# Attention logits and indexer scores computed for two heads per step, one head on each half of TensorE's rows

## The chip, the cores and the metric

One core of one Trainium2 chip runs the whole kernel. The metric is the device time of one launch in microseconds (us). TensorE (PE) multiplies, and its weight loads have a row of their own (PEld); VectorE (DVE), ScalarE (ACT) and GpSimd (POOL) do the rest, and SyncE (SP) issues the weight DMAs.

## The reference, cut to what matters

A trunk of two layers over 528 positions (16 meta tokens and 512 tokens) of width 1024, in float32. Layer 0 is RWKV-7 time mixing, layer 1 sparse attention; each is wrapped in two SwiGLU feed-forwards. The change is in layer 1 alone. There, `q` has 16 heads of 64, `k` and `v` 4 heads of 64, and a small indexer has 8 query heads `qi` of 64, one key `ki` and 8 weights `wi`:

```python
rel = relu(einsum("bqhd,bkd->bqhk", qi, ki))
score = einsum("bqh,bqhk->bqk", wi, rel)          # then causal mask
_, idx = top_k(score, 128)
logits = einsum("bqgrd,bqkgd->bqgrk", qg, kg) * 64 ** -0.5
p = softmax(logits over the 128 selected keys)
o = einsum("bqgrk,bqkgd->bqgrd", p, vg)
```

## The kernel before, in words

**The dense part.** Each weight block of 128 columns is split into a rounded part and a rest (`Weights.round` on ACT, `Weights.split` on DVE; tiles `whi` and `wlo`, 1024 columns at a time), each activation likewise, and a block product is three matmuls in a rounded format (`mm3`, line 496) into a bank of the tag `acc` (four buffers). The stages are generators that yield before each block; `ffn` (614), `kvq` (1545) and `ao` (1650) are such main streams.

**The side work.** Attention and the indexer run as side chains (`beside`, 711) that `run` (729) mixes into a main stream while the program is built. `Clock` (238) holds a time for every engine by a price list; a matmul of float32 operands is priced at four passes over its columns, one matmul after another. Before each main block `run` lets chains step whose inputs are due earlier, and after it chains that are ready, until TensorE's modelled time has grown by `share` = 400 ns, as long as the modelled DVE and ACT are no more than `FULL` ahead (1500 ns beside `kvqA` and `f10b`, 3000 ns beside `kvqB` and `f11a`, line 47 and 732). A chain that yields `("bg", a, b)` is ready when the next buffer of the tag `bg` and the tiles `a`, `b` are free in the model (`Clock.late`, 285): one buffer is looked at, the next. `drain` (750) steps chains that are left over when a main stream ends. The order so fixed is the order on the chip; each engine executes its own in order.

**Banks.** `bbank` (493) hands out PSUM banks for side work: tag `bg` in a ring of three, `ry` one.

**The indexer**, `select(i)` (1467), for the query block i = 0 to 3 of 128 tokens, with `Wd` = 144 + 128 i keys in two halves `s`: for each of 8 heads and each half, one yield, one float32 matmul of 64 rows (`qiT[i][half, c]` against `kiT[half, s]`; even heads lie on partitions 0 to 63, odd ones on 64 to 127, and `kiT` is on both) into one `bg` bank, a relu on ACT into `rel[:, s]`, and a multiply-add on DVE into `sc`. Then 16 rounds of max and replace on DVE make the selection, and `bias[i]`.

**Attention**, `attend(i)` (1570), i = 1 to 4, with `Wd` = 16 + 128 i keys: `logits(hh)` (1579) makes, for each segment of the keys (one, or two of 264 at i = 4), one float32 matmul of 64 rows into one `bg` bank, and a DVE operation that adds the bias out of the bank into `pr` and takes the minimum; then ACT takes the exponential. `divide(hh)` (1597) normalises on DVE. `turn(hh)` (1602) transposes the head's probabilities by TensorE into a `bg` bank (two of them at i = 4), and DVE and ACT copy them into `pt`. `values(g)` (1620) multiplies by V for four heads at once. The loop at line 1639 runs `logits(s)`, `divide(s - 1)`, `turn(s - 3)`, so a head is turned three heads after its logits.

**Where it runs.** `select(0)`, `select(1)` and `attend(1)`, `attend(2)` lie beside `kvqA` and the feed-forward `f10b`; `select(2)`, `select(3)`, `attend(3)`, `attend(4)` beside `kvqB` and `f11a` (lines 1695 to 1714). After each feed-forward comes `drain`, then `ao`, which needs attention's result.

Of the kernel before, what the change touches and what calls it, by code (L numbers as in the profile page):

```python
# [10 lines left out]
F32 = mybir.dt.float32  # L11
F32R = mybir.dt.float32r
I32 = mybir.dt.int32
AF = mybir.ActivationFunctionType
OP = mybir.AluOpType
# [4 lines left out]
T = 528  # L20
# [413 lines left out]
def trunk(ctx, tc, wall, units, h0, vec, cstd, gqk, out, stop=None, gap=0.0, share=400.0, slack=200.0, fulls={}):  # L434
    clock = Clock()
    nc = Core(tc.nc, clock)
    @contextmanager
    def tile_pool(name, bufs=1, **kw):
        with tc.tile_pool(name=name, bufs=bufs, **kw) as pool:
            yield Pool(pool, bufs, clock)  # L440
# [52 lines left out]
    def bbank(tag="bg"):  # L493
        return psum.tile([128, 512], F32, name=tag, bufs={"bg": 3, "ry": 1}[tag])
# [870 lines left out]
    at = ctx.enter_context(tile_pool("at"))  # L1365
# [24 lines left out]
    for q in ("cos", "sin"):  # L1390
        turns[2, q] = cst[q].rearrange("p (i e) -> p i e", e=16)
        for w in range(2):
            turns[w, q] = at.tile([128, 5, 16], F32, name=f"{q}{w}")
            nc.vector.tensor_tensor(turns[w, q], turns[2, q], gb[:, w:w + 1, 0:16].to_broadcast([128, 5, 16]),
                                    op=OP.mult)
    kT = at.tile([128, 4, T], F32, name="kT")
    V = at.tile([128, 5, 256], F32, name="V")
    kiT = at.tile([128, T], F32, name="kiT")
    qiT = {}
    wi = at.tile([128, 4, 8], F32, name="wi")  # L1400
    qT = {}
# [60 lines left out]
    def segments(Wd):  # L1462
        return [(0, Wd)] if Wd <= 512 else [(0, Wd // 2), (Wd // 2, Wd)]

    bias = {}

    def select(i):

        Wd = 144 + 128 * i
        sc = at.tile([128, T], F32, name="sc", bufs=1)  # L1470
        rel = at.tile([128, T], F32, name="rel", bufs=1)
        for hh in range(8):
            c, half = hh // 2, slice(64 * (hh % 2), 64 * (hh % 2) + 64)
            for s in (slice(0, Wd // 2), slice(Wd // 2, Wd)):
                yield "bg", qiT[i][half, c], kiT[half, s]
                p = bbank()[:, :Wd // 2]
                nc.tensor.matmul(p, qiT[i][half, c], kiT[half, s], start=True, stop=True)
                nc.scalar.activation(rel[:, s], p, AF.Relu)
                if hh == 0:
                    nc.vector.tensor_scalar(sc[:, s], rel[:, s], wi[:, i, 0:1], None, op0=OP.mult)  # L1480
                else:
                    nc.vector.scalar_tensor_tensor(sc[:, s], rel[:, s], wi[:, i, hh:hh + 1], sc[:, s],
                                                   op0=OP.mult, op1=OP.add)
        nc.vector.tensor_add(sc[:, Wd - 128:Wd], sc[:, Wd - 128:Wd], cst["causal"])
        wk = at.tile([128, T], F32, name="rel", bufs=1)
        m8 = at.tile([128, 8], F32, name="m8", bufs=1)
        for t in range(TOPK // 8):
            src = sc if t == 0 else wk
            nc.vector.max(m8, src[:, :Wd])
            nc.vector.match_replace(out=wk[:, :Wd], in_to_replace=m8, in_values=src[:, :Wd], imm_value=-2.0 * BIG)  # L1490
            yield -1500
        b = at.tile([128, T], F32, name=f"bias{i % 2}")
        nc.vector.tensor_scalar(b[:, :Wd], wk[:, :Wd], -1.5 * BIG, BIG, op0=OP.is_gt, op1=OP.mult)
        nc.vector.scalar_tensor_tensor(b[:, Wd - 128:Wd], cst["causal"], -1.0, b[:, Wd - 128:Wd],
                                       op0=OP.mult, op1=OP.max)
        bias[i] = b
# [73 lines left out]
    def attend(i, XO):  # L1570


        Wd = 16 + 128 * i
        nb = i + 1
        b = bias[i - 1]
        sm = at.tile([128, 16], F32, name="sm", bufs=1)
        pr, pt, po = {}, {}, {}

        def logits(hh):

            c, half, g = hh // 2, slice(64 * (hh % 2), 64 * (hh % 2) + 64), hh // 4
            lg = pr[hh] = at.tile([128, T], F32, name="pr", bufs=4)
            mn = at.tile([128, 2], F32, name="mn", bufs=4)
            sg = segments(Wd)
            for j, (s0, s1) in enumerate(sg):
                yield "bg", qT[i][half, c], kT[half, g, s0:s1]
                p = bbank()
                nc.tensor.matmul(p[:, :s1 - s0], qT[i][half, c], kT[half, g, s0:s1], start=True, stop=True)
                nc.vector.tensor_tensor_reduce(out=lg[:, s0:s1], in0=p[:, :s1 - s0], in1=b[:, s0:s1],
                                               scale=1.0, scalar=3e38, op0=OP.add, op1=OP.min,  # L1590
                                               accum_out=mn[:, j:j + 1])
            if len(sg) == 2:
                nc.vector.tensor_tensor(mn[:, 0:1], mn[:, 0:1], mn[:, 1:2], op=OP.min)
            nc.scalar.activation(lg[:, :Wd], lg[:, :Wd], AF.Exp, bias=mn[:, 0:1], scale=-1.0,
                                 accum_out=sm[:, hh:hh + 1])

        def divide(hh):
            r = sm[:, hh:hh + 1]
            nc.vector.reciprocal(r, r)
            nc.vector.tensor_scalar(pr[hh][:, :Wd], pr[hh][:, :Wd], r, None, op0=OP.mult)  # L1600

        def turn(hh):
            if hh % 4 == 0:
                pt[hh // 4] = at.tile([128, 5, 4, 128], F32, name="pt", bufs=1)
            to = pt[hh // 4][:, :, hh % 2 * 2 + hh % 4 // 2]
            for k0 in range(0, nb, 4):
                ks = range(k0, min(k0 + 4, nb))
                yield "bg", pr[hh][:, :Wd]
                p = bbank()
                pv = p.rearrange("p (m t) -> p m t", t=128)  # L1610
                for kb in ks:
                    t0, t1 = TOK[kb]
                    nc.tensor.transpose(pv[:t1 - t0, kb - k0], pr[hh][:, t0:t1], ident)
                if k0 == 0:
                    nc.vector.tensor_copy(to[:16, 0], pv[:16, 0])
                    nc.scalar.activation(to[:, 1:len(ks)], pv[:, 1:len(ks)], AF.Copy)
                else:
                    nc.scalar.activation(to[:, k0:k0 + len(ks)], pv[:, :len(ks)], AF.Copy)

        def values(g):  # L1620

            q, c0 = g // 2, 256 * (g % 2)
            yield "ry" if g % 2 == 0 else po[q][:, c0:c0 + 256], pt[g]
            if g % 2 == 0:
                po[q] = bbank("ry")
            for kb in range(nb):
                k = TOK[kb][1] - TOK[kb][0]
                for o in (0, 1):
                    nc.tensor.matmul(po[q][64 * o:64 * o + 64, c0:c0 + 256], V[:k, kb, 64 * g:64 * g + 64],
                                     pt[g][:k, kb, 2 * o:2 * o + 2].rearrange("p h t -> p (h t)"),  # L1630
                                     start=kb == 0, stop=kb == nb - 1)
            if g % 2:
                pv = po[q].rearrange("p (m t) -> p m t", t=128)
                s = slice(TOK[i][0] - XO.t0, TOK[i][1] - XO.t0)
                hi, lo = XO.hi[:, 4 * q:4 * q + 4, s], XO.lo[:, 4 * q:4 * q + 4, s]
                nc.scalar.activation(hi, pv, AF.Copy)
                nc.vector.tensor_sub(lo, pv, hi.bitcast(F32))

        for s in range(20):
            if s % 4 == 3 and s > 3:  # L1640
                yield from values(s // 4 - 1)
            if s < 16:
                yield from logits(s)
            if 0 <= s - 1 < 16:
                divide(s - 1)
            if 0 <= s - 3 < 16:
                yield from turn(s - 3)
        yield 0

    def ao(XO, r, nxt, X=None):  # L1650
# [21 lines left out]
    def attend_range(q, i, name):  # L1672
        while ("q", i + 1) not in have or i - 1 not in bias:
            yield None
        XO[q] = Split(xq, DT, q, name)
        yield from attend(i, XO[q])
        while i not in bias:
            yield None
        yield from attend(i + 1, XO[q])
# [15 lines left out]
    QI = tiles_of((1, 2, 0), "xb_hi")  # L1695
    run(early(idx(XS["xa"], QI, (0, 1, 2)), norms[3], B))
    beside(heads_chain(), chain(*(idx_heads(i, QI) for i in (0, 1, 2)), select(0), select(1)))
    beside(attend_range(QA, 1, "xa"))
    run(early(kvq(XS["xa"], (0, 1, 2)), norms[3], B, X=x_of(B, "xb"), start=40), "kvqA")
# [4 lines left out]
    QI = tiles_of((3, 4), "xa_hi")  # L1704
    run(early(idx(XS["xb"], QI, (3, 4)), norms[5], QA))
    beside(heads_chain(), chain(idx_heads(3, QI), idx_heads(4, QI), select(2), select(3)))
    beside(attend_range(QB, 3, "xb"))
    run(early(kvq(XS["xb"], (3, 4)), norms[5], QA, X=x_of(QA, "xa"), start=40), "kvqB")
# [63 lines left out]
```

## Time and profile before

| what | us |
|---|---|
| median of 3 runs | 2402.96 (2399.5 to 2404.71) |
| the profiled execution | 2405.28 |
| its span on the core | 2403.5 |
| TensorE matmul busy | 2335.7 |
| VectorE busy | 1706.2 |
| ScalarE busy | 1263.9 |

The profiled execution is one launch; its span runs from its first to its last instruction. A float32 matmul stands in the trace as two MATMUL records and two weight loads. Every operation is recorded under the line of one helper, L341, so tile names tell the groups apart: `bg<-kT,qT` is a logits matmul, `bg<-kiT,qiT` a score matmul, `bg<-ident,pr` a transpose of `turn`, `ry<-pt,V` one of `values`, and `acc<-...` the main stream. A MATMUL's duration reaches to its modelled end, so neighbours overlap; what a matmul costs TensorE is read from starts.

### The profile page before, as it was taken

How to read it: one execution, taken by the hardware profiler on the slowest of the kernel's cores; microseconds unless marked ns; L12 is line 12 of the kernel's file. 1: busy time of each engine (PE TensorE's matmuls, PEld its weight loads, DVE VectorE, ACT ScalarE, POOL GpSimd, SP SyncE). 2: the span in 40 equal slices, each digit the busy share in tenths (PEclk: the TensorE clock that was granted, in tenths of full speed). 3: DMA queues.
4: the chain of work that ended last, by engine and by line, in shares of the span. 5: the costliest groups of instructions: out<-in, count | busy, mean ns of one | idle time of the engine just before them, and what ended most of it. 6: DMA issues, size and time to landing. Idle time of an engine off the chain costs nothing.

```text
span 2403.5 us, 49406 instructions
## 1 busy us (share of the span) xinstructions
PE 2335.7 (97%) x20122; PEld 2189.8 (91%) x20122; DVE 1706.2 (71%) x3337; ACT 1263.9 (53%) x2125; POOL 169.5 (7%) x215
## 2 busy tenths in 40 slices
PE   8998999999889999999999999999999999999999
PEld 8997889998789899999999999799888888879999
DVE  7667888856787975576566566687767888666765
ACT  5443664456448535644444444456665546565543
POOL 0001521010043011000000000000000000000000
PEclk9999999999899999999999999999999999999999
DMA  6553335542334454244555555454434444425554
GB/s 228 174 177 114 125 125 172 172 133 72 106 115 159 153 164 133 81 132 153 176 176 167 186 190 177 140 168 142 150 122 138 141 144 133 139 78 168 177 185 141
DMA packets 101491, 356.13 MB, mean 148 GB/s; under 512 B 11520, under 2 KB 15632, under 8 KB 101264
## 3 DMA queue, kind: packets, MB, share of 16 engines
q1 hardware_dynamic: 99120, 347.91, 43.8%
q0 software_dynamic: 2144, 5.07, 0.8%
q8 instruction: 158, 2.59, 0.4%
q14 instruction: 69, 0.57, 0.1%
HBM read 348.60 MB, written 4.33 MB: 147 GB/s over the span
## 4 chain that ended last, share of the span: by engine, by line
PE 53%; DVE 2%; ACT 1%; issue 0%; DVEq 0%; ACTq 0%
PE acc L341 46%; PE bg L341 6%; PE ry L341 1%; DVE wlo L341 1%; DVE qst L341 0%; ACT whi L341 0%; DVE h L341 0%; DVE pr L341 0%; DVE tb L341 0%; DVE xa_lo L341 0%; DVE m L341 0%; DVE rel L341 0%; DVE nst L341 0%; DVE hid_lo L341 0%; ACT xa_hi L341 0%
## 5 line engine op out<-in xcount | busy, mean ns | idle before, releaser
L341 ACT ACTIVATE whi<-wraw 128x1024 fp32r<-128x1024 f32 (+1 forms) x658 | 688.5, 1051 | 465.2 <-PE acc L341 274.8
L341 DVE TENSOR_TENSOR wlo<-wraw,whi 128x1024 fp32r<-128x1024 f32 (+1 forms) x658 | 809.8, 1234 | 170.8 <-ACT whi L341 170.1
L341 PE MATMUL acc<-hid_hi,whi 128*128 128x256 f32 (+1 forms) x1408 | 412.1, 293 | 6.0 <-DVE h L341 5.9
L341 PE MATMUL acc<-hid_lo,whi 128*128 128x256 f32 (+1 forms) x1408 | 399.5, 284 | 0.0
L341 PE MATMUL acc<-hid_hi,wlo 128*128 128x256 f32 (+1 forms) x1408 | 399.4, 284 | 0.0
L341 PE MATMUL acc<-xa_hi,whi 128*128 128x256 f32 (+1 forms) x1088 | 316.4, 291 | 1.8 <-ACT xa_hi L341 1.4
L341 PE MATMUL acc<-x_hi,whi 128*128 128x272 f32 (+1 forms) x1024 | 303.1, 296 | 8.7 <-ACT whi L341 6.2
L341 PE MATMUL acc<-xa_hi,wlo 128*128 128x256 f32 (+1 forms) x1088 | 309.0, 284 | 0.1
L341 PE MATMUL acc<-xa_lo,whi 128*128 128x256 f32 (+1 forms) x1088 | 308.9, 284 | 0.1
L341 PE MATMUL acc<-x_hi,wlo 128*128 128x272 f32 (+1 forms) x1024 | 294.9, 288 | 0.5 <-DVE wlo L341 0.5
L341 PE MATMUL acc<-x_lo,whi 128*128 128x272 f32 (+1 forms) x1024 | 294.5, 288 | 0.1
L341 PEld LDWEIGHTS acc<-hid_hi,whi 128*128 128x128 f32 x1408 | 265.5, 189 | 23.0 <-issue 12.2
L341 PEld LDWEIGHTS acc<-hid_lo,whi 128*128 128x128 f32 x1408 | 266.9, 190 | 0.2 <-DVE hid_lo L341 0.2
L341 PEld LDWEIGHTS acc<-hid_hi,wlo 128*128 128x128 f32 x1408 | 265.8, 189 | 0.0
L341 PEld LDWEIGHTS acc<-xa_hi,whi 128*128 128x128 f32 x1088 | 206.2, 190 | 19.7 <-issue 17.1
L341 PE MATMUL acc<-xb_hi,whi 128*128 128x256 f32 x752 | 215.4, 286 | 0.0
L341 PE MATMUL acc<-xb_lo,whi 128*128 128x256 f32 x752 | 210.7, 280 | 0.0
L341 PE MATMUL acc<-xb_hi,wlo 128*128 128x256 f32 x752 | 210.6, 280 | 0.0
L341 PEld LDWEIGHTS acc<-x_hi,whi 128*128 128x128 f32 x1024 | 194.9, 190 | 15.2 <-ACT whi L341 6.2
L341 PEld LDWEIGHTS acc<-xa_lo,whi 128*128 128x128 f32 x1088 | 206.6, 190 | 0.6 <-DVE xa_lo L341 0.5
L341 PEld LDWEIGHTS acc<-xa_hi,wlo 128*128 128x128 f32 x1088 | 206.2, 190 | 0.4 <-DVE wlo L341 0.4
L341 PEld LDWEIGHTS acc<-x_hi,wlo 128*128 128x128 f32 x1024 | 194.7, 190 | 1.0 <-DVE wlo L341 1.0
(295 smaller groups left out, 4440.4 us busy)
## 6 DMA issues: line engine op xcount, KB each, us to landing
wraw<-wall SPq DMA_DIRECT2D x644, 512.0 KB, 3.3
wraw<-wall SPq DMA_DIRECT2D x10, 438.0 KB, 3.3
out<-h SPq DMA_DIRECT2D x8, 256.0 KB, 2.3
h<-h SPq DMA_DIRECT2D x2, 512.0 KB, 8.7
ynat<-L POOLq DMA_DIRECT2D x2, 512.0 KB, 4.4
T<-ynat POOLq DMA_DIRECT2D x2, 512.0 KB, 4.2
L<-gm POOLq DMA_DIRECT2D x14, 64.0 KB, 2.8
gm<-T POOLq DMA_DIRECT2D x4, 224.0 KB, 6.8
```

Of the source, the lines that this page charges most:

```text
L341: r = f(*args, **kw)
```

## The change

`select` handles two heads `2c`, `2c + 1` per step and half of the keys: one yield (on both heads' rows), two banks, the two matmuls one right behind the other, then two relus and two multiply-adds. The relus write two slots of `rel` by head, no longer by half of the keys. `logits(c)` does the same for two heads and each segment: one yield, two banks, two matmuls, two DVE operations; then minima and exponentials of both. The loop of `attend` runs over 8 pairs: `logits(c)`, `divide` of both heads of c - 1, `turn` of both heads of c - 1, and `values` after every second pair. The rings (three `bg` banks, four `pr` and `mn` buffers), the price list and the yields' check of one next buffer stay.

```diff
+        w = Wd // 2
+        for c in range(4):
+            for s in (slice(0, w), slice(w, Wd)):
+                yield "bg", qiT[i][:, c], kiT[:, s]
+                ps = [bbank()[:, :w] for _ in range(2)]
+                for o in (0, 1):
+                    half = slice(64 * o, 64 * o + 64)
+                    nc.tensor.matmul(ps[o], qiT[i][half, c], kiT[half, s], start=True, stop=True)
+                for o in (0, 1):
+                    hh, r = 2 * c + o, rel[:, o * w:(o + 1) * w]
+                    nc.scalar.activation(r, ps[o], AF.Relu)
...
-        def logits(hh):
+        def logits(c):
...
+            for o in (0, 1):
+                pr[2 * c + o] = at.tile([128, T], F32, name="pr", bufs=4)
+                mn[o] = at.tile([128, 2], F32, name="mn", bufs=4)
             for j, (s0, s1) in enumerate(sg):
-                yield "bg", qT[i][half, c], kT[half, g, s0:s1]
-                p = bbank()
-                nc.tensor.matmul(p[:, :s1 - s0], qT[i][half, c], kT[half, g, s0:s1], start=True, stop=True)
-                nc.vector.tensor_tensor_reduce(out=lg[:, s0:s1], in0=p[:, :s1 - s0], in1=b[:, s0:s1],
-                                               scale=1.0, scalar=3e38, op0=OP.add, op1=OP.min,
-                                               accum_out=mn[:, j:j + 1])
+                yield "bg", qT[i][:, c], kT[:, g, s0:s1]
+                ps = [bbank()[:, :s1 - s0] for _ in range(2)]
+                for o in (0, 1):
+                    half = slice(64 * o, 64 * o + 64)
+                    nc.tensor.matmul(ps[o], qT[i][half, c], kT[half, g, s0:s1], start=True, stop=True)
+                for o in (0, 1):
+                    nc.vector.tensor_tensor_reduce(out=pr[2 * c + o][:, s0:s1], in0=ps[o], in1=b[:, s0:s1],
+                                                   scale=1.0, scalar=3e38, op0=OP.add, op1=OP.min,
+                                                   accum_out=mn[o][:, j:j + 1])
...
-        for s in range(20):
-            if s % 4 == 3 and s > 3:
-                yield from values(s // 4 - 1)
-            if s < 16:
-                yield from logits(s)
-            if 0 <= s - 1 < 16:
-                divide(s - 1)
-            if 0 <= s - 3 < 16:
-                yield from turn(s - 3)
+        for c in range(9):
+            if c % 2 and c > 1:
+                yield from values(c // 2 - 1)
+            if c < 8:
+                yield from logits(c)
+            if c:
+                for hh in (2 * c - 2, 2 * c - 1):
+                    divide(hh)
+                for hh in (2 * c - 2, 2 * c - 1):
+                    yield from turn(hh)
+        yield from values(3)
```

## Rows read from the trace of the kernel before

**Rows 1.** The page: the span, and busy time, share and count of each engine.

```profile
span 2403.5 us, 49406 instructions
...
PE 2335.7 (97%) x20122; PEld 2189.8 (91%) x20122; DVE 1706.2 (71%) x3337; ACT 1263.9 (53%) x2125; POOL 169.5 (7%) x215
```

**Rows 2.** Busy time by stretch: start:end, length, then PE, PEld, DVE, ACT, POOL.

```profile
1962.00:1982.00 20.00, 20.00 (x91) 12.39 (x90) 12.43 (x23) 8.59 (x21) 0.00 (x0) 1.00 0.29 97
...
1520.00:1811.00 291.00, 288.50 (x2071) 252.31 (x2070) 213.18 (x560) 177.05 (x320) 0.10 (x1) 0.99 0.42 141
1860.00:2187.00 327.00, 323.40 (x2200) 266.75 (x2199) 245.71 (x594) 188.59 (x324) 0.00 (x0) 1.00 0.39 127
```

**Rows 3.** Tile views of qT, then qiT: count, ns min/median/max, starts, forms.

```profile
L341 PE MATMUL bg<-kT,qT x160: 282/438/601, 1642.8 to 2169.2; 64*128 64x264 f32 x64, 64*128 64x144 f32 x32, 64*128 64x272 f32 x32, 64*128 64x400 f32 x32
...
L341 PE MATMUL bg<-kiT,qiT x128: 272/329/487, 1526.8 to 1981.4; 64*128 64x72 f32 x32, 64*128 64x136 f32 x32, 64*128 64x200 f32 x32, 64*128 64x264 f32 x32
```

**Rows 4.** Timeline of PE, one logits matmul of 144 columns: start, us, instruction.

```profile
1642.23 0.28 PE L341 MATMUL acc<-xb_hi,wlo 128*128 128x256 f32 x1
...
1642.58 0.28 PE L341 MATMUL acc<-xb_hi,wlo 128*128 128x256 f32 x1
1642.79 0.51 PE L341 MATMUL bg<-kT,qT 64*128 64x144 f32 x2
...
1643.45 0.28 PE L341 MATMUL acc<-xb_lo,whi 128*128 128x256 f32 x1
```

**Rows 5.** Timeline of PE, one logits matmul of 400 columns.

```profile
1990.84 0.28 PE L341 MATMUL acc<-xa_hi,wlo 128*128 128x256 f32 x1
1991.04 0.94 PE L341 MATMUL bg<-kT,qT 64*128 64x400 f32 x2
...
1992.13 0.28 PE L341 MATMUL acc<-xa_lo,whi 128*128 128x256 f32 x1
```

**Rows 6.** Timeline of PE, two logits matmuls of 400 columns in a row.

```profile
2000.35 0.28 PE L341 MATMUL acc<-xa_hi,wlo 128*128 128x256 f32 x1
2000.55 0.94 PE L341 MATMUL bg<-kT,qT 64*128 64x400 f32 x4
...
2001.65 0.28 PE L341 MATMUL acc<-xa_lo,whi 128*128 128x256 f32 x1
```

**Rows 7.** Timeline of PE, two score matmuls of one head, 136 columns each.

```profile
1624.06 0.28 PE L341 MATMUL acc<-xb_hi,wlo 128*128 128x256 f32 x1
1624.27 0.73 PE L341 MATMUL bg<-kiT,qiT 64*128 64x136 f32 x4
...
1625.15 0.28 PE L341 MATMUL acc<-xb_lo,whi 128*128 128x256 f32 x1
```

**Rows 8.** Groups of ACT and DVE, 1520 to 2190: busy us, mean ns, idle before.

```profile
L341 ACT ACTIVATE whi<-wraw 128x1024 fp32r<-128x1024 f32 (+1 forms) x171 | 177.9, 1047 | 49.3 <-PE acc L341 32.9 <-DVE q L341 5.5 <-issue 4.5
...
L341 ACT ACTIVATE pt<-bg 128x384 f32<-128x384 f32 (+2 forms) x80 | 28.8, 382 | 35.2 <-DVE pt L341 32.5 <-DVE sm L341 2.0
L341 ACT ACTIVATE rel<-bg 128x72 f32<-128x72 f32 (+3 forms) x64 | 19.3, 311 | 30.5 <-PE bg L341 27.5 <-DVE bias L341 2.4
...
L341 DVE TENSOR_TENSOR wlo<-wraw,whi 128x1024 fp32r<-128x1024 f32 (+1 forms) x170 | 205.6, 1213 | 24.4 <-ACT whi L341 24.3
L341 DVE CUSTOM_DVE_ANT_0 pr<-bg,bias 128x264 f32<-128x264 f32 (+3 forms) x80 | 34.7, 434 | 41.0 <-PE bg L341 40.9
```

**Rows 9.** Waits of PEld, 1520 to 2190: total us, times, longest.

```profile
PEld bg L341 <- DVE mn L341: 1.8, 6, 0.6
PEld bg L341 <- ACT pt L341: 1.1, 3, 0.5
```

**Rows 10.** Timeline of PE: the last `values` before `ao`, and the first block of `ao`.

```profile
1807.10 1.66 PE L341 MATMUL ry<-pt,V 16*64 16x256 f32 x12
...
1811.27 0.28 PE L341 MATMUL acc<-xa_hi,whi 128*128 128x256 f32 x1
```

More of the change, by code (lines that the diff above doesn't have):

```diff
@@ L1471, in select @@
         rel = at.tile([128, T], F32, name="rel", bufs=1)
[L1472 to L1483, printed above, removed]
+        w = Wd // 2
[9 more added lines that the diff above has]
+                    nc.scalar.activation(r, ps[o], AF.Relu)
+                    if hh == 0:
+                        nc.vector.tensor_scalar(sc[:, s], r, wi[:, i, 0:1], None, op0=OP.mult)
+                    else:
+                        nc.vector.scalar_tensor_tensor(sc[:, s], r, wi[:, i, hh:hh + 1], sc[:, s],
+                                                       op0=OP.mult, op1=OP.add)
         nc.vector.tensor_add(sc[:, Wd - 128:Wd], sc[:, Wd - 128:Wd], cst["causal"])
@@ L1577, in attend @@
         pr, pt, po = {}, {}, {}
-        def logits(hh):
-            c, half, g = hh // 2, slice(64 * (hh % 2), 64 * (hh % 2) + 64), hh // 4
-            lg = pr[hh] = at.tile([128, T], F32, name="pr", bufs=4)
-            mn = at.tile([128, 2], F32, name="mn", bufs=4)
+        def logits(c):
+            g = c // 2
+            mn = {}
+            for o in (0, 1):
+                pr[2 * c + o] = at.tile([128, T], F32, name="pr", bufs=4)
+                mn[o] = at.tile([128, 2], F32, name="mn", bufs=4)
             sg = segments(Wd)
             for j, (s0, s1) in enumerate(sg):
-                yield "bg", qT[i][half, c], kT[half, g, s0:s1]
-                p = bbank()
-                nc.tensor.matmul(p[:, :s1 - s0], qT[i][half, c], kT[half, g, s0:s1], start=True, stop=True)
-                nc.vector.tensor_tensor_reduce(out=lg[:, s0:s1], in0=p[:, :s1 - s0], in1=b[:, s0:s1],
-                                               scale=1.0, scalar=3e38, op0=OP.add, op1=OP.min,
-                                               accum_out=mn[:, j:j + 1])
[L1592 to L1595, printed above, removed]
+                yield "bg", qT[i][:, c], kT[:, g, s0:s1]
[7 more added lines that the diff above has]
+                                                   accum_out=mn[o][:, j:j + 1])
+            for o in (0, 1):
+                lg = pr[2 * c + o]
+                if len(sg) == 2:
+                    nc.vector.tensor_tensor(mn[o][:, 0:1], mn[o][:, 0:1], mn[o][:, 1:2], op=OP.min)
+                nc.scalar.activation(lg[:, :Wd], lg[:, :Wd], AF.Exp, bias=mn[o][:, 0:1], scale=-1.0,
+                                     accum_out=sm[:, 2 * c + o:2 * c + o + 1])
         def divide(hh):
```

## The prediction, made before the changed kernel was run

> **What bounds the kernel.** I read the page first: matmuls fill 97% of the span and VectorE 71% [rows 1], so TensorE comes first in question. The stretches where the changed code runs say the same more sharply: 288.5 of 291 us and 323.4 of 327 us of TensorE are busy, VectorE 213.2 and 245.7 [rows 2]. So in these two stretches TensorE sets the pace, its work is one stream in program order, and whatever a side matmul takes out of that stream the main matmuls get back. The tile views give the number of side matmuls: two records each, so 80 for logits and 64 for scores, all on 64 rows [rows 3]. What one costs must be read from starts, not from durations, and for that I took timelines of single places.
>
> **The price of one matmul.** Main matmuls start 0.117 us apart (1642.23 to 1642.58 for three) [rows 4]. Around a logits matmul of 144 columns, the last main start before it and the second main start behind it lie 0.87 us apart; less two normal steps, it took 0.64 us out of the stream [rows 4]. One of 400 columns took 1.29 - 0.23 = 1.06 us [rows 5]. The 256 further columns cost 0.42 us, 1.64 ns each; so each visit has a fixed price of 0.64 - 144 x 1.64 ns = 0.40 us, paid for leaving the main stream and coming back. By this line 264 columns cost 0.83 us, 272 cost 0.85, 200 cost 0.73, 136 cost 0.62 and 72 cost 0.52.
>
> **What a second head on the other half costs.** The trace has one place where the planner by chance put two heads' logits behind each other: four records of 400 columns, an even and an odd head. They took 1.30 - 0.23 = 1.07 us [rows 6], against 1.06 for one [rows 5]. So the second head cost 0.01 us: no fixed price and no columns. Two matmuls on the same half are different: two of 136 columns, of one head, took 1.09 - 0.23 = 0.86 us [rows 7], that is 0.62 and the second one's 0.22 in full, with the fixed price paid once.
>
> The Trainium skill (TensorE: Matmul & The Clock Gate, Part 3, The mechanism) says that matmuls on different row groups overlap, but also that matmuls start and end strictly in program order. Taken literally for the two records of each matmul, only one's second record could lie beside the other's first, and a pair would stream three halves of one matmul; by that the sum would be 13 us smaller. The four records of the trace end with those of a single matmul, so here the trace does not agree, and I go by it.
>
> **The change part by part.** *Logits*: 80 matmuls become 40 pairs, and a pair costs TensorE what one does, plus 0.01. Saved are 8 x 0.64 = 5.1 us at i = 1, 8 x 0.85 = 6.8 at i = 2, 8 x 1.06 = 8.4 less the 1.1 of the place that is paired already = 7.3 at i = 3, and 16 x 0.83 = 13.3 at i = 4: together 32 us after the 0.01 each.
>
> *Scores*: at i = 3 the 16 visits become 8, saving 8 x 0.83 = 6.7 us. At i = 1 and 2 the planner already puts a head's two halves into one visit (eight visits like the one of [rows 7]); a pair's modelled price is now over its 400 ns, so I expect one pair to a visit: 8 x (0.86 - 0.63) = 1.8 us, and at 200 columns 8 x (0.40 + 2 x 0.33 - 0.74) = 2.5 us. At i = 0 the saving is 0.9 us with one pair to a visit and 2.5 with two; I take 1.5. Together 12.5 us.
>
> *ScalarE and VectorE* have the same operations on the same columns: cost nothing beside TensorE, as VectorE would then be busy some 459 of 573 us in the two stretches, 80% [rows 2]. In the scores of i = 3 that cover is thin: 12.4 us of VectorE in 20 us [rows 2], and the stretch loses about 7, so VectorE nears its limit there.
>
> *Turns and divides* move: a head is turned one pair behind its logits instead of three heads, so a turn now waits for two additions (0.43 us each [rows 8]) and its own divide. The planner knows this wait and puts main blocks in between; it costs the chain time, not TensorE's.
>
> *Banks.* This is the added wait. The ring keeps three banks, the pair takes two, and the yield asks for the first alone. For scores the second bank is the previous pair's first, which has to be read by a relu (0.31 us); for logits it is that of the turn before, read by copies (0.38 us); both may sit behind a rounding of weights, 1.05 us on ScalarE or 1.21 us on VectorE [rows 8]. Behind the waiting matmul stands the whole main stream. Today such waits hardly exist: the two largest are 1.8 and 1.1 us in all [rows 9]. The nearest rows bound the new ones: no wait more than now (nothing), and at the other end each of 72 pairs behind a full rounding and its copy, less the time that one main block (three starts, 0.35) and half of the fixed price (0.20) give it: 1.05 + 0.38 - 0.35 - 0.20 = 0.88 us, 63 us in all. A gain below nothing is excluded, as no bank comes free earlier. I take a third of the pairs, 24, each with half a rounding, 0.55 us: 13 us. It is nearer the low end, since ScalarE is idle for some 40% of both stretches [rows 2] and the waits of today are so small.
>
> Sum: 32 + 12.5 - 13 = 31.5 us saved. The profiled execution took 2405.3 us (1.8 around its span of 2403.5), 2.3 above the median of 2403.0; against the median I get **2371 us**.
>
> **Rivals.** *The halves take turns* (the change doesn't do what it says): pairs save the fixed price only, 39 x 0.40 for logits and 8 x 0.40 for the scores of i = 3, 19 us, less 13 of waits: 2397. Against it stand [rows 5, 6]; for it only that this is a single place. Chance 0.05. *Only half of each pair overlaps*: the 72 pairs hold 10752 + 5376 columns, 26 us of streaming; half is 13, so 2384. The same rows speak against it. Chance 0.06. It is what the skill's rule of strict order would make, and the trace does not bear it out.
>
> *The chain sets the end*: the feed-forward beside `attend(2)` outlasts attention by only 2.5 us (its last values end at 1808.76, `ao` begins at 1811.27) [rows 10]. If attention's own latency, through VectorE, doesn't shrink with TensorE's time, the 15 us saved by then (5.1 + 6.8 + 1.8 + 1.5) come back but for 2.5 as a drained chain: 2371 + 12.5 = 2383. For it: the later divide-to-turn order; against it: 16 fewer steps to fit in, and VectorE idle for 27% of that stretch [rows 2]. Chance 0.10.
>
> *Slower: the second bank is late each time.* If nearly every pair meets the 0.88 us worked out above, 63 us of waits stand against 44.5 saved: 2421. It decides from 44.5 / 72 = 0.62 us a pair. For it: the yield looks at one bank, and the planner lets VectorE and ScalarE run 1.5 to 3 us ahead; against it: most pairs have at least a main block and a turn between bank and reuse. Chance 0.10. The skill (TensorEngine Tiling (Array Packing), PSUM Bottleneck) warns in this sense that packing speeds TensorE but not the reading of PSUM, which may become the bottleneck; no row of this trace shows that yet.
>
> **How the numbers follow.** My forecast keeps 0.69, its own range being 2357 (few waits) to 2385. A measurement of this kernel tells about 0.2%, 5 us, from no change. The range from 2355 to 2392 takes in the forecast, the chain and the half overlap, and leaves out the late banks and the halves that take turns, and tails of the forecast. Faster by over 0.2% (below 2398): 0.69 + 0.10 + 0.06 and most of 0.05, less a little for the forecast's upper tail, 0.87. Within 0.2%: 0.04. Slower: 0.09.
>
> **What would show it.** Right: the timeline shows four records of logits within the time of two now, some 1.07 us out of the stream at 400 columns; LDWEIGHTS of `bg` waiting for `rel`, `pt` or `mn` by some 13 us in all; `acc` groups unchanged in number; TensorE's busy share still near 97%. The terms are wrong if a pair takes more than 0.1 us over a single one, or if the waits on banks exceed 25 us. The forecast falls if TensorE stands idle ahead of `ao` for more than a few us (the chain), or if those waits exceed 44 us.

## The result and the profile after

The kernel after takes 2375.19 us (median of 4 runs, 2369.8 to 2381.21) against 2401.23 us (4 runs) for the kernel before: ratio 0.9896, 95% interval 0.9873 to 0.992. A second measurement (e5 below) gave 0.9873 (0.9852 to 0.9894). The profiled execution took 2373.61 us. So the kernel is faster by some 25 to 30 us; 2371 was forecast, in a range of 2355 to 2392.

The page of after, the span and the busy times, which answer to [rows 1]:

```profile
span 2371.8 us, 49461 instructions
...
PE 2298.7 (97%) x20122; PEld 2172.6 (92%) x20122; DVE 1702.1 (72%) x3337; ACT 1238.7 (52%) x2109; POOL 169.6 (7%) x215
```

The span is 31.7 us shorter, TensorE's busy time 37.0 us, with the same 20122 matmul records: more of them lie on top of each other. VectorE has the same work to 4 us. ScalarE has 16 instructions and 25.2 us less: a pair's two exponentials now follow each other, which saves table loads (shown at the end).

**Pairs.** The timeline of TensorE in after, at a pair of logits of 400 columns, which answers to [rows 5, 6]:

```profile
1957.30 0.28 PE L341 MATMUL acc<-xa_hi,wlo 128*128 128x256 f32 x1
1957.51 0.94 PE L341 MATMUL bg<-kT,qT 64*128 64x400 f32 x4
1958.39 0.38 PE L341 MATMUL acc<-xa_hi,whi 128*128 128x256 f32 x1
1958.61 0.28 PE L341 MATMUL acc<-xa_lo,whi 128*128 128x256 f32 x1
```

From 1957.30 to 1958.61 are 1.31 us; less two normal steps of 0.117 us, the pair took 1.07 us out of the main stream. A single one took 1.06 before. The same view at two score matmuls of 136 columns, now two heads, which answers to [rows 7]:

```profile
1620.37 0.28 PE L341 MATMUL acc<-xb_hi,wlo 128*128 128x256 f32 x1
1620.57 0.50 PE L341 MATMUL bg<-kiT,qiT 64*128 64x136 f32 x4
1621.01 0.38 PE L341 MATMUL acc<-xb_hi,whi 128*128 128x256 f32 x1
1621.23 0.28 PE L341 MATMUL acc<-xb_lo,whi 128*128 128x256 f32 x1
```

Four records now take 0.50 us where four took 0.73 us, and 0.63 us out of the stream where it was 0.86. Read in the same way, the undisturbed pairs took 0.64 us at 144 columns, 0.85 at 272 and 0.84 at 264.

**Waits.** The waits of TensorE's weight loads in after, 1520 to 2160 us (engine, line, waited for: total, times, longest), which answer to [rows 9]:

```profile
PEld bg L341 <- ACT pt L341: 9.9, 11, 2.7
...
PEld bg L341 <- ACT rel L341: 4.3, 11, 0.5
```

Before, the same two rows held 1.1 and 0.9 us. Whose they are is told by the tile views of the weight loads (the total in us and the times), first `qT`, the logits:

```profile
L341 PEld LDWEIGHTS bg<-kT,qT x160: 182/184/187, 1642.5 to 2119.0; 64*128 64x128 f32 x160
...
  ACT pt L341: 3.2, 5
```

then `qiT`, the scores:

```profile
L341 PEld LDWEIGHTS bg<-kiT,qiT x128: 182/184/187, 1526.3 to 1955.7; 64*128 64x128 f32 x128
...
  ACT rel L341: 4.3, 11
```

and `pr`, the transposes of the turns:

```profile
L341 PEld LDWEIGHTS bg<-ident,pr x224: 86/139/146, 1667.9 to 2127.7; 128*128 128x128 f32 x64, 128*16 128x16 f32 x48
...
  ACT pt L341: 6.8, 6
```

The three are not alike. Each of the five waits of the logits stands ahead of a pair's second matmul: 3.2 us for the pair's second bank. What one costs shows the timeline of TensorE in after at a late pair of 144 columns:

```profile
1689.47 0.28 PE L341 MATMUL acc<-xb_hi,wlo 128*128 128x256 f32 x1
1689.68 0.51 PE L341 MATMUL bg<-kT,qT 64*128 64x144 f32 x2
1690.46 0.51 PE L341 MATMUL bg<-kT,qT 64*128 64x144 f32 x2 [0.27 <-ACT pt L341]
1690.90 0.38 PE L341 MATMUL acc<-xb_hi,whi 128*128 128x256 f32 x1
1691.12 0.28 PE L341 MATMUL acc<-xb_lo,whi 128*128 128x256 f32 x1
```

From 1689.47 to 1691.12, less two steps, it took 1.42 us where an undisturbed pair takes 0.64. Its second weight load waited 0.48 us; the other 0.30 us are about the second head's own 144 columns (0.24 us at 1.64 ns), which no longer lay beside the first head's.

The scores' 4.3 us are nearly all no wait for a bank. Ten of the eleven stand ahead of a pair's first matmul, and there the relu had ended 0.15 to 0.42 us before the load. The timelines at 200 columns, first of before, then of after (the second row of before and the last of after are the first weight loads of a visit):

```profile
1865.36 0.40 PE L341 MATMUL acc<-wlo,xb_hi 128*128 128x512 f32 x1
1865.68 0.63 PEld L341 LDWEIGHTS bg<-kiT,qiT 64*128 64x128 f32 x4 [0.36 <-issue]
```

```profile
1848.15 0.57 ACT L341 ACTIVATE rel<-bg 128x200 f32<-128x200 f32 x2 [0.63 <-PE bg L341]
1848.62 0.39 PE L341 MATMUL acc<-wlo,xb_hi 128*128 128x512 f32 x1
1848.94 0.30 PEld L341 LDWEIGHTS bg<-kiT,qiT 64*128 64x128 f32 x4 [0.36 <-ACT rel L341]
```

The load comes 0.32 us behind the last main matmul in both, with the same 0.36 us of idle before it, which the view of before puts down to no one and that of after to a relu that was over at 1848.72. It is the way out of a main stream of 512 columns, and these pairs cost 0.73 us, as forecast for 200 columns. One score pair of the eleven had a late second bank (0.46 us, at 1955.62).

So the pair's second bank was late for 6 of 72 pairs, 3.6 us of waits, and by their visits the six cost some 5 us over undisturbed pairs (for the one that shares its visit with a turn this is an estimate). The largest wait belongs to the turns, which the change only moved.

**The end of attention.** The timeline of TensorE in after: the last `values` of `attend(2)`, the first block of `ao`, the last `values` of `attend(4)` and the first block of the next `ao`, which answer to [rows 10]:

```profile
1786.46 1.66 PE L341 MATMUL ry<-pt,V 16*64 16x256 f32 x12
...
1796.80 0.28 PE L341 MATMUL acc<-xa_hi,whi 128*128 128x256 f32 x1
...
2129.01 2.52 PE L341 MATMUL ry<-pt,V 16*64 16x256 f32 x20
...
2155.04 0.28 PE L341 MATMUL acc<-xb_hi,whi 128*128 128x256 f32 x1
```

Attention's last matmul now starts 9.1 and 23.8 us ahead of `ao`; before it was 2.9 us at the first place.

**Where the time went.** In these two traces the whole difference lies between the first score matmul and the second `ao`, as the starts of the timelines show. Stretch A reaches from the first score matmul to the first `ao`, stretch B from there to the second `ao`; the end behind it is 215 to 218 us in every kernel. Lead is the time from the start of the last matmul of the last `values` to `ao`. Each row is one profiled execution; the two kernels that stand here twice differ by 2.4 and 2.0 us from themselves, and the 31.1 us of after are some 3 to 5 us more than the medians above give.

| kernel | A, us | B, us | sum against before | lead at A, B |
|---|---|---|---|---|
| before | 284.5 | 375.3 | | 2.9, 7.9 |
| after | 270.5 | 358.2 | -31.1 | 9.1, 23.8 |
| e5 after, again | 272.1 | 359.0 | -28.7 | 9.0, 23.9 |
| e1 same half | 277.7 | 372.2 | -9.9 | 9.1, 23.9 |
| e3 logits alone | 276.6 | 360.6 | -22.6 | 6.1, 0.3 |
| e4 scores alone | 282.4 | 368.0 | -9.4 | 0.6, 8.0 |
| e6 order alone | 292.7 | 382.0 | +14.9 | 0.6, 0.3 |
| e9 before, look-up mended | 288.6 | 386.9 | +15.7 | 0.3, 0.3 |
| e2 both banks asked for | 272.3 | 355.3 | -32.2 | 0.3, 0.5 |
| e8 both banks, more ahead | 268.7 | 353.5 | -37.6 | 17.8, 24.5 |
| e7 next bank asked for | 270.5 | 349.1 | -40.2 | 9.0, 11.4 |
| e10 e7 again | 272.1 | 349.5 | -38.2 | 9.1, 11.4 |

**A fact of the planner** that neither the views of before nor the forecast had. `Clock.late` looks a bank up under the bare tag `bg`, but the model counts PSUM tiles under longer names that begin with `bg_psum`. So the look-up finds nothing, in both kernels: the yield does not ask for the next bank, as the description above has it from the code, but for none. That the names matter is seen in e7, where the look-up by the full name alone changes the order and the time.

### The profile page after: what moved, and what is told of

Same layout as the page of the kernel before. It is cut to its first block, busy times and chain, and to the rows that moved or that the text cites. A ratio compares the mean times of both kernels' runs of the same rounds, so it can differ in the third digit from the quotient of the medians.

```text
span 2371.8 us, 49461 instructions
## 1 busy us (share of the span) xinstructions
PE 2298.7 (97%) x20122; PEld 2172.6 (92%) x20122; DVE 1702.1 (72%) x3337; ACT 1238.7 (52%) x2109; POOL 169.6 (7%) x215
## 4 chain that ended last, share of the span: by engine, by line
PE 48%; DVE 5%; ACT 2%; issue 1%; ACTq 0%; DVEq 0%
PE acc L341 43%; PE bg L341 4%; DVE wlo L341 2%; PE ry L341 1%; ACT whi L341 1%; DVE pr L341 0%; DVE m L341 0%; ACT L341 0%; DVE rel L341 0%; DVE tb L341 0%; ACT pr L341 0%; DVE qst L341 0%; DVE h L341 0%; DVE xa_lo L341 0%; ACT pt L341 0%
```

## The experiments

### e1: both matmuls on one half of the rows

```diff
-                    half = slice(64 * o, 64 * o + 64)
+                    half = slice(0, 64)
```

The edit stands in `select` and in `logits`. Each pair's second matmul takes the even head's rows, so the odd heads' scores and logits are left out; instructions, banks and order are those of after.

> The changed kernel, but both matmuls of a pair run on rows 0 to 63 (the odd head's logits and scores are left out, the even head's are made twice); the order of every engine stays the same. Theory A (two halves run beside each other): the second matmul of a pair now costs its columns, 16128 of them at 1.64 ns, 26 us; up to 8 us of that is taken back, since longer visits leave fewer waits for banks: 2393 to 2401 us, and one pair of 400 columns takes 1.07 + 0.66 = 1.73 us out of the stream. Theory B (the gain comes from fewer visits alone): 2375, as the changed kernel.

Measured: 2387.37 us, ratio 0.9955 (0.9934 to 0.9975). The timeline of TensorE in e1, at the same kind of pair as above:

```profile
1963.28 0.28 PE L341 MATMUL acc<-xa_hi,wlo 128*128 128x256 f32 x1
1963.49 1.61 PE L341 MATMUL bg<-kT,qT 64*128 64x400 f32 x4
1965.03 0.39 PE L341 MATMUL acc<-xa_hi,whi 128*128 128x256 f32 x1
1965.26 0.28 PE L341 MATMUL acc<-xa_lo,whi 128*128 128x256 f32 x1
```

From 1963.28 to 1965.26, less two steps: 1.74 us, 0.67 us more than on two halves. So it is the other half of the rows that makes the second head free, not the matmuls' neighbourhood. The time lies between the two theories' values: the two stretches are 21.2 us longer than after's, where 26 us of columns stream one after another. Added up over their visits, the scores take 8.7 us more than in after, which is their 5376 columns at 1.64 ns (8.8 us); so the `rel` row's fall from 4.3 to 0.9 us gave no time back. Attention's visits take 12.1 us more, where its 10752 columns make 17.6. While the second matmul streams, banks come free: the waits for `pt` fall from 9.9 to 6.0 us, and 21.2 with these 3.9 added is 25.1, about the columns' 26.

### e3 and e4: the logits alone, the scores alone

e3 is after with `select` of before; e4 is after with `logits` and the loop of `attend` of before. The edits against after, cut, first e3's, then e4's:

```diff
-        for c in range(4):
-            for s in (slice(0, w), slice(w, Wd)):
+        for hh in range(8):
...
-        for c in range(9):
+        for s in range(20):
```

> Attention's logits in pairs as in the changed kernel, the indexer's scores one head at a time as before. Theory A (each part gives what its visits saved): 12 us of the scores are lost again, 2387 (2383 to 2391). Rival (the scores' gain is swallowed by the waits that it brings): 2375.

> The indexer's scores in pairs, attention one head at a time in the old order. Theory A: 12 us gained against before, less some 2 us of waits for relus: 2391 (2388 to 2394). Rival (the scores' gain is swallowed): 2401, as before.

Measured: e3 2376.02 us, ratio 0.9907 (0.9886 to 0.9927); e4 2389.2 us, 0.9955 (0.9938 to 0.9972). The stretches give -22.6 and -9.4 us, which add up to -32.0 where both together give -31.1. The parts don't disturb each other, and the logits bring more than two thirds. By its time e3 came out where the rival had it (2375). But its profiled execution reached the first score matmul at 1518.8 us, after's at 1526.3, in a stage that no edit touches; by the stretches the scores gain 8.5 us on top of the logits, and in e4 they gain 9.3 us alone by the medians. So the rival falls by these two, and not by e3's time.

### e2: the look-up mended, both banks asked for

```diff
-            tag, bufs = out, self.bufs.get(out, 1)
-            _, list_ = self.seen.get((tag, (self.count.get(tag, -1) + 1) % bufs), (None, []))
-            t = max((e[0] for e in list_ if e[6] != "tensor"), default=0.0)
+            name = out.rstrip("2"); tag = next((k for k in self.bufs if k.startswith(name + "_psum")), name)
+            at = [(self.count.get(tag, -1) + k) % self.bufs.get(tag, 1) for k in (1, 2)[:1 + (out != name)]]
+            t = max((e[0] for k in at for e in self.seen.get((tag, k), (0, []))[1] if e[6] != "tensor"), default=0.0)
...
-                yield "bg", qT[i][:, c], kT[:, g, s0:s1]
+                yield "bg2", qT[i][:, c], kT[:, g, s0:s1]
```

The yield of `select` asks for `bg2` as well.

> The changed kernel with a planner whose yields really look up when bg banks come free, both banks of a pair included (in both kernels the look-up finds nothing, as the buffers are counted under a longer name). Theory A1 (TensorE waits for banks because the planner doesn't know that they are late): the waits of bg matmuls for pt and rel copies, 14 us in the changed kernel, fall under 6 us, and the time to 2363 to 2371. Theory A2 (the planner's times for ScalarE are too short, or the lost time lies elsewhere): waits stay above 10 us and the time between 2372 and 2380.

Measured: 2367.86 us, ratio 0.9874 (0.9854 to 0.9895), within A1's times, with 7.1 us in the two rows of waits where A1 had under 6. The rows, 1520 to 2200 us:

```profile
PEld bg L341 <- ACT rel L341: 4.2, 9, 0.9
...
PEld bg L341 <- ACT pt L341: 2.9, 7, 1.0
```

The wait for `pt` falls from 9.9 to 2.9 us, that for `rel`, mostly no wait, stays, and the two stretches gain 1.1 us only, less than two executions of one kernel differ by. Attention, put off more often, now ends right at both `ao` (leads 0.3 and 0.5), and what is left of it runs with no main blocks between. So two effects seem to stand against each other here, and the run by itself does not price the banks.

### e5 and e6: after again, and its order alone

e5 is the kernel after. e6 has the scores of before and after's order of attention (two heads' logits, both divides, both turns), but each head's logits with a yield and a bank of its own. Against after, cut, and without the scores:

```diff
-            for j, (s0, s1) in enumerate(sg):
-                yield "bg", qT[i][:, c], kT[:, g, s0:s1]
-                ps = [bbank()[:, :s1 - s0] for _ in range(2)]
...
+            for o in (0, 1):
+                half = slice(64 * o, 64 * o + 64)
+                for j, (s0, s1) in enumerate(sg):
+                    yield "bg", qT[i][half, c], kT[half, g, s0:s1]
+                    p = bbank()[:, :s1 - s0]
```

> The changed kernel itself once more, on the chip of the runs beside it, to be compared with them: 25 to 31 us under the kernel before, ratio 0.987 to 0.990. If the logits alone already give all of the gain (rival from the run of the logits alone, 0.9907), it stands no lower than 0.9905.

> The changed kernel's order of attention (logits of two heads, divides and turns of the pair before), but each head's logits matmul with a yield and a bank of its own, and the scores as before, one head at a time. Theory A (the gain is that of the paired visits): within 5 us of the kernel before, ratio 0.998 to 1.002; where the planner puts two heads behind each other by itself, up to 5 us less. Rival (the new order itself gives or costs time): under 0.994 or over 1.004.

Measured: e5 2374.54 us, ratio 0.9873 (0.9852 to 0.9894). e6 2418.81 us, ratio 1.007 (1.0051 to 1.0089): the order by itself makes the kernel slower, by 14.9 us in the two stretches. The tile view of e6's weight loads for the transposes:

```profile
L341 PEld LDWEIGHTS bg<-ident,pr x224: 86/139/230, 1668.8 to 2193.8; 128*128 128x128 f32 x64, 128*16 128x16 f32 x48
...
  ACT pt L341: 6.7, 8
  DVE pr L341: 2.8, 1
```

The 6.7 us on `pt` are after's 6.8, with no pair in the kernel: they belong to the order, and the 2.8 us on `pr` to the divide that now lies just ahead of its turn. Of the rest, a part is at the ends: e6 has a lead of 0.6 and 0.3 us, and its drained `turn` and `values` run with nothing between them. Another part is the clock: in e6's two stretches it was granted at 0.50 for 27.3 us, in before's for 6.8 and in after's for 10.2. How the 14.9 us divide among these stays open. By the leads in the table after doesn't pay the part at the ends.

### e7 and e10: the look-up mended for the one next bank

The edit is e2's in `Clock.late`, with the yields left at `"bg"`.

> The changed kernel with the planner's look-up of banks mended, but for the next bank alone. Theory A1 (the pair's second bank is what is late): waits of bg matmuls for pt and rel stay near the 14 us of the changed kernel, and the time within 4 us of it. Rival (any honest look-up does it): waits under 7 us, and 4 us or more under the changed kernel.

> The same kernel as e7_ask_next_bank, a second time, on another call: the kernel after with the look-up of the one next bank mended. Theory A: its 12 us over the kernel after are there again: ratio to the kernel before 0.982 to 0.987, and TensorE waits for the turns' transposes under 1 us in attention's region. Rival B: the gain was one chip's or one call's clock: ratio 0.988 to 0.991, as the kernel after.

Measured: e7 2362.65 us, ratio 0.984 (0.9819 to 0.9861), 12 us under e5, which ran beside it; e10 2363.5 us, 0.9847 (0.9828 to 0.9866). The tile view of the weight loads for the transposes in e7:

```profile
L341 PEld LDWEIGHTS bg<-ident,pr x224: 86/139/146, 1665.6 to 2128.6; 128*128 128x128 f32 x64, 128*16 128x16 f32 x48
...
  ACT pt L341: 0.2, 1
```

From 6.8 us to 0.2, while the logits keep 3.1 us and the scores' row its 4.3: what the mended look-up takes away is not the pair's second bank, but the turns' own. The theory that the second bank is the one that matters falls; the rival has the time right, with 7.6 us in the two rows of waits where it had under 7. Stretch A is the same as after's; B is 9.1 us shorter. Of these 6.6 us are the turns' waits, and 1.7 us a lower clock, which is told at the end. This is the fastest version of the study.

### e8: both banks asked for, more work ahead

e2's kernel with more modelled VectorE and ScalarE work allowed ahead, so that attention is not put off to the ends:

```diff
-FULL = {"pA": 2000.0, "pB": 1500.0, "f01a": 1500.0, "kvqA": 1500.0, "f10b": 1500.0, "f11a": 3000.0}
+FULL = {"pA": 2000.0, "pB": 1500.0, "f01a": 1500.0, "kvqA": 1500.0, "f10b": 2500.0, "f11a": 4500.0}
```

> The planner asks for both banks of a pair, and beside f10b and f11a VectorE and ScalarE may be planned 2.5 and 4.5 us ahead in place of 1.5 and 3.0, so that attention is done before the feed-forwards end and no chain is drained. Theory A1: without the drained ends of the run that asks for both banks (some 8 to 12 us of idle TensorE there), and with few waits for banks, 2356 to 2364 us beside 2398, ratio 0.983 to 0.986. Rival (more planned ahead brings the waits back): as the changed kernel, 0.988 to 0.991.

Measured: 2368.36 us, ratio 0.9862 (0.9841 to 0.9884), slower than was expected and the same as e2. The leads are back (17.8 and 24.5 us) and the stretches gain 5.4 us over e2; but its profiled run reached the first score matmul at 1532.9 us, e2's at 1522.2, so that part of the gain is covered by an earlier stage of the program. That stage holds the same 13774 matmul records in both; in e8 the granted clock was 0.50 for 105.8 us of it, in e2 for 81.9. The 23.9 us more at half the clock are worth up to 12 us, an estimate from these figures, and the stage took 10.7 us longer. The edit changes nothing in that stage.

### e9: the look-up mended in the kernel before

The edit is e2's in `Clock.late`, made in the kernel before (cut):

```diff
-            tag, bufs = out, self.bufs.get(out, 1)
...
+            name = out.rstrip("2"); tag = next((k for k in self.bufs if k.startswith(name + "_psum")), name)
...
```

> The kernel before with one edit: the planner's look-up of a background bank finds the bank that comes next, by its full name. Everything else, the single heads and their order, is the kernel before's. Theory A: mending the look-up is worth time only where a bank is often late, which the pairs and the moved turns of the kernel after make (TensorE's waits on background banks in attention's region: 4.6 us before, 23.0 after, 10.6 with the look-up mended); before it there is little to win, 4.6 us at most, and steps that are put off leave more of attention to the drained ends of the two regions. Expected: ratio to the kernel before 0.998 to 1.012. Rival B: the look-up is worth the same 10 to 12 us in either kernel: ratio 0.994 to 0.997.

Measured: 2416.68 us, ratio 1.0062 (1.0044 to 1.008), as theory A has it: the look-up is not worth 10 us by itself. (The 23.0 us of waits in the expectation add those of the weight loads and those of the matmuls behind them, which are in part the same time.) Its second end, by stretch (start:end, length, then busy time of PE, PEld, DVE, ACT and POOL, granted clock, DMA share, GB/s), and below it the same of the kernel before:

```profile
2155.00:2199.00 44.00, 40.04 (x157) 21.67 (x157) 17.68 (x77) 15.66 (x44) 0.00 (x0) 0.65 0.02 7
```

```profile
2143.00:2187.00 44.00, 43.28 (x306) 33.42 (x305) 24.71 (x70) 27.90 (x51) 0.00 (x0) 1.00 0.31 102
```

For 44 us TensorE has only attention to do, 157 matmuls where the kernel before has 306 in as long a time, and the granted clock is 0.65. Before had leads of 2.9 and 7.9 us in which a step could be put off, after 9.1 and 23.8; that this is why the same edit costs time here and gains it there fits the table, and was not tried by itself.

## Why the prediction was right, point by point

**TensorE's pace**: right. The stretches are 31.1 us shorter, where 31.5 was forecast, and TensorE's busy share is still 97%. By the medians of all runs the gain is 26.0 us, and 27.8 in e5.

**A pair costs what a single matmul does**: right, with 1.07 us at 400 columns and 0.63 at 136. e1 shows that this is the halves' doing. Both rivals of the halves fall, the turns (2397) and the half overlap (2384). The Trainium skill (TensorE: Matmul & The Clock Gate, Part 3, The mechanism) has matmuls start and end strictly in program order. In e1 the four records of a pair signal behind the second and the fourth, so they run head by head; in after they start at 1957.51, 1957.52, 1957.95 and 1957.96, and the last two signal, so the heads' first records run together and then their second ones. Record by record this does not agree with the rule; taken matmul by matmul nothing in these rows is against it. The prediction's 13 us less by that rule did not come.

**Logits 32 us, scores 12.5 us**: right. Added up over all visits of the two stretches (as in [rows 4], from the last main start before a visit to the second one behind it, less two normal steps), the scores took 35.3 us of the stream before and 23.1 after, 12.2 less. Logits, turns and `values` often share a visit; together they took 124.7 us before and 105.4 after, 19.3 less, which makes 31.5 with the scores. In e7, where the turns hardly wait, they took 96.5, 28.2 less; with some 4 us that its late pairs cost, this is the forecast's 32.

**Bank waits 13 us**: right in size, and not where the forecast put them. The pair's second bank was late for 6 pairs and cost some 5 us, where the forecast had 24 pairs and 13 us. The waits' own rows, 14.2 us, come close to 13 only because they hold 3.8 us of the scores that are no waits.

**The step that failed** is inside that sum: "Turns and divides move ... it costs the chain time, not TensorE's". At i = 4 the two turns of a pair ask for four banks from a ring of three, one behind the other, and the last waits for ScalarE's copy of the first. The transposes' waits for `pt` grew from 0.6 to 6.8 us (e6 shows them with no pair, e7 takes them away), and e7's stretches say that the moved turns cost some 9 us. So a term of 0 was 9 us, and one of 13 was 5: two errors of about the same size, in opposite directions, made the sum right, and that is luck. Behind the first stood a reading of the code: the yield was taken to ask for one bank, and it asks for none, so the planner does not see the turns' late bank. The second was a guess at how many pairs come late.

**The chain sets the end** (2383): fell. The lead at the first end grew from 2.9 to 9.1 us. That is the planner's order, not the columns saved: e1, which streams all the columns in after's order, has the same lead, and e6, with after's order of attention and a yield for each head, has 0.6. The rival's mechanism is real, though: e6, e9 and e2 have it, and e9's stretches are 15.7 us longer.

**The second bank late each time** (2421): fell, with 6 of 72 pairs. The Trainium skill (TensorEngine Tiling (Array Packing), PSUM Bottleneck) warns that packing speeds up TensorE and not the reading of PSUM, which may become the bottleneck. In this trace it did not: reads of PSUM held back these six pairs, 3.6 us of waits in all.

## What to carry to other kernels

Two float32 matmuls of 64 rows on the two halves of the array cost here as much as one, and if they were single visits in a stream of other matmuls they also share one visit's fixed price: read both from starts, not from durations. When a change regroups the work, price each group's demand on every ring (here four banks from three, two steps away from the edit), and not only that of the instructions that were edited. Hold a wait against the end of what it is put down to: if that was long over, nobody waited for it. And see that a planner's question finds what it asks for: an answer "free" for a name that nobody counts looks like a bank that is never late.

## What the runs showed of the hardware

A single long wait of TensorE can cost more than itself. The timeline of TensorE in after, at the worst wait of a turn, and `values` behind it (idle before and its releaser in brackets):

```profile
2070.33 1.15 PE L341 MATMUL bg<-ident,pr 128*16 128x128 f32 x9
2073.90 0.33 PE L341 MATMUL bg<-ident,pr 128*128 128x128 f32 x1 [2.43 <-ACT pt L341]
...
2075.22 4.21 PE L341 MATMUL ry<-pt,V 16*64 16x256 f32 x20
```

and the granted clock by stretch, columns as in e9:

```profile
2072.00:2073.00 1.00, 0.00 (x0) 0.00 (x0) 0.52 (x3) 0.89 (x2) 0.00 (x0) 1.00 0.78 274
...
2075.00:2076.00 1.00, 1.00 (x9) 0.48 (x9) 0.00 (x0) 0.86 (x1) 0.00 (x0) 0.92 0.43 86
2076.00:2077.00 1.00, 1.00 (x6) 0.56 (x6) 0.00 (x0) 0.00 (x0) 0.00 (x0) 0.50 0.78 283
2077.00:2078.00 1.00, 1.00 (x8) 0.47 (x6) 0.00 (x0) 0.00 (x0) 0.00 (x0) 0.50 0.41 160
```

TensorE stood idle for 2.43 us, at full granted clock; it was busy again from 2073.90, and some two microseconds later the clock fell to 0.50, the lower of its two levels. The `values` there took 4.21 us, where the same work at 2129.01 took 2.52 (above). So the wait cost 2.4 us and 1.7 us more behind it. In e5, the same kernel, the same wait of 2.43 us stands there, the clock fell as well, and the `values` took 4.46 us. In e7, without that wait, the `values` of this place took 2.52 us. Their rows, e5 first, then e7:

```profile
2076.70 4.46 PE L341 MATMUL ry<-pt,V 16*64 16x256 f32 x20
```

```profile
2073.16 2.52 PE L341 MATMUL ry<-pt,V 16*64 16x256 f32 x20
```

Not every wait does this in every execution: at the late pair of 400 columns near 2000 us TensorE stood idle for 0.76 to 0.78 us in after, e5, e7 and e10 alike; shortly behind it the granted clock was 0.50 in e5 and e10 and 1.00 in after and e7.

ScalarE's table loads were not in the forecast, which had ScalarE's work unchanged. From 1520 to 2190 us, before and then after (busy us, mean ns, idle before):

```profile
L341 ACT ACT_TABLE_LOAD x45 | 57.7, 1283 | 0.8
```

```profile
L341 ACT ACT_TABLE_LOAD x30 | 38.5, 1283 | 0.5
```

Two exponentials in a row share a load: 19.2 us less of ScalarE's time. TensorE sets the pace here; what these loads were worth in time was not tried.
